# RWKV's three sums over a head (key norm, mean, variance): a pair of rounded products in place of one fp32 product

## The chip, the core and the metric

One core of a Trainium2 chip runs the whole program. The metric is the device time of one execution in microseconds; the kernel before was timed in 3 runs. Every instruction is recorded by the hardware profiler in one further execution.

## The reference, cut to what matters

The program is one inference step of a two-layer streaming encoder for a prompt of 512 tokens and 8 sequences of 16 tokens, 640 tokens in all. Layer 0's mixer runs RWKV-7 time mixing (8 heads of 64) beside forgetting attention (8 heads of 64) on one input projection; an output projection joins them. What the change touches is in RWKV, in three sums over the 64 channels of a head:

```python
    kk = k * k_k.reshape(H_A, HEAD_DIM).astype(jnp.float32)
    kk = kk / jnp.maximum(jnp.sqrt(jnp.sum(kk * kk, axis=-1, keepdims=True)), 1e-12)
...
    y, s_t = wkv7_scan(r, decay, k, v, -kk, kk * a, s0)
    mean = jnp.mean(y, axis=-1, keepdims=True)
    var = jnp.mean(jnp.square(y - mean), axis=-1, keepdims=True)
    y = (y - mean) * lax.rsqrt(var + GN_EPS) * lnx_g.reshape(H_A, HEAD_DIM).astype(jnp.float32) \
        + lnx_b.reshape(H_A, HEAD_DIM).astype(jnp.float32)
```

Everything is fp32. The later layers (a gated convolutional FFN after each mixer, chunk attention beside HGRN2 in layer 1's mixer) are not touched.

## The kernel before, in words

Activations lie with channels on the 128 partitions and tokens along the free axis, in two halves of 320 tokens. A large projection is `linear` (line 362): each weight tile of 128x1024 is loaded, split by ScalarE into a rounded part `whi` (L376) and by VectorE into what remains, `wlo` (L377), and each output tile is the sum of three rounded products per tile of the contraction, (whi, hi), (whi, lo), (wlo, hi), all on line 387 with 320 columns. These L387 products are most of TensorE's work.

Layer 0's mixer is `mixer0` (line 545). Its input projection feeds `evz` (line 893), which collects r, k and v of a pair of heads and then calls `rwkv` (line 617) for that pair and half: 8 items in all, one for each of four pairs `p` and two halves `hf`. An item has three stages. Stage A forms decays, the normed key `kk`, masks and the products `sc`; stage B inverts a triangular system (a part of it on POOL, by way of DRAM); stage C carries the state, makes `y` (tile `Y`, L836), takes its mean and variance, scales it and writes it to DRAM (`ydr`, L888). Each stage has its own ring of buffers of 320 columns, 11 for A, 8 for B and 5 for C (line 624); a buffer is taken when a tile is made and given back after its last reader. The buffer `ABM`, which holds `AR`, `BK` and the masked products of an item, is there twice, so an item uses that of the item two before it.

A sum over a head is a product with a matrix that has ones in two blocks of 64x64 (`blkr`). In `rwkv` it is `m1` (line 634), one fp32 product (L636). Layer 1's HGRN2 takes its one sum by `headsum` (line 224): its caller has ScalarE write the rounded part `sh` (L1383), VectorE subtracts it (`sl`, L226), and two rounded products accumulate (L228).

Attention over the prompt and the samples comes after the input projection in the program, in a lane of its own. Then `out_proj` (line 531) runs twice: first with attention's outputs, then with RWKV's four `ydr` tiles. It reads each tile back (`yb`, L538), rounds it (`yh`, L539) and subtracts (`yl`, L540). The second one does all output tiles for the first half of the tokens, then all for the second half.

No order is written by hand. Code is assigned to lanes with priorities (`k.lane`), and a scheduler lists the instructions of every engine by priority and by when it takes their inputs and buffers to be ready. Each engine then runs its list in that order. A new instruction or a longer lifetime of a buffer can therefore move others.

Of the kernel before, what the change touches and what calls it, by code (L numbers as in the profile page):

```python
# [12 lines left out]
AF = mybir.ActivationFunctionType  # L13
ALU = mybir.AluOpType
# [530 lines left out]
def mixer0(tc, A, k):  # L545
    nc = tc.nc
    V, S, G, T, dma, mm, fm, P, C = k.V, k.S, k.G, k.T, k.dma, k.mm, k.fm, k.P, k.C
    ident, blk1, one = k.ident, k.blk1, k.one
# [8 lines left out]
    with tc.tile_pool(name="mx", bufs=1) as mp:  # L557
# [59 lines left out]
        def rwkv(p, hf, r, kz, v, lrt, grt, item):  # L617
# [5 lines left out]
            def wt(name, w=HF, dt=F32):  # L623
                return mp.tile([128, w], dt, tag="w" + stage[0], name=name, bufs={"A": 11, "B": 8, "C": 5}[stage[0]])

            def hsum(src, t, func, name, **kw):
                hi, lo = wt("hi", dt=F32R), wt("lo", dt=F32R)
                S.activation(hi, src, func, **kw)
                return k.headsum(mm(name, stage[0]), t, hi, lo)
# [4 lines left out]
            def m1(lhsT, rhs, name):  # L634
                ps = mm(name, stage[0])
                T.matmul(ps[:, 0:HF], lhsT, rhs, start=True, stop=True)  # L636
                return ps[:, 0:HF]
# [5 lines left out]
            kk, rn = wt("kk"), wt("rn")  # L643
            V.tensor_scalar(kk, kz, P("k_k", p), None, op0=ALU.mult)
            S.activation(rn, kz, AF.Square, scale=P("k_k", p))
            ps = m1(blk1, rn, "kkn")
            n2, rn = wt("n2"), wt("rn")
            V.tensor_scalar(n2, ps, 1e-24, None, op0=ALU.max)
            S.activation(rn, n2, AF.Ln, scale=float(2 ** 20))
# [32 lines left out]
            for (u0, n, prompt) in (((0, 4, 1), (4, 1, 1)) if hf == 0 else ((0, 3, 1), (3, 2, 0))):  # L682
                for h in range(2):
                    ps = mm("sc", stage[0])
# [59 lines left out]
            ps = mm("trA", stage[0])  # L744
# [4 lines left out]
            ps = mm("trV", stage[0])  # L749
# [7 lines left out]
            for (u0, n) in ((0, 4), (4, 1)):  # L757
                ps = mm("trB", stage[0])
# [18 lines left out]
            ps = mm("U", stage[0])  # L777
# [27 lines left out]
            y = wt("y")  # L805
# [7 lines left out]
            for c in range(npu):  # L813
# [6 lines left out]
                ps = mm("Sn", stage[0])  # L820
# [8 lines left out]
            ps = mm("Y", stage[0])  # L829
# [8 lines left out]
            if hf:  # L838
# [4 lines left out]
                ps = mm("SAs", stage[0])  # L843
# [12 lines left out]
                ps = mm("Ss", stage[0])  # L856
# [9 lines left out]
                ps = mm("Ys", stage[0])  # L866
# [8 lines left out]
                S.copy(y[:, 192:320], ps[:, 0:128])  # L875
                dma(A["o_rw"][:, p], rwo)

            V.scalar_tensor_tensor(y, m1(blk1, y, "mean"), -1.0 / 64, y, op0=ALU.mult, op1=ALU.add)
            sq = wt("sq2")
            S.activation(sq, y, AF.Square)  # L880
            rs = wt("rs")
            S.activation(rs, m1(blk1, sq, "var"), AF.Ln, scale=1.0 / 64, bias=k.gneps)
            S.activation(rs, rs, AF.Exp, scale=-0.5)
            V.tensor_tensor(y, y, rs, op=ALU.mult)
            V.tensor_scalar(y, y, P("lnx_g", p), P("lnx_b", p), op0=ALU.mult, op1=ALU.add)
# [7 lines left out]
        def evz(m, h, ps):  # L893
# [24 lines left out]
            if m == 12:  # L918

                t = o[0:64]  # L920
                V.tensor_scalar(t, t, 2.0, None, op0=ALU.mult)
                sigm(t, t, None)
                V.tensor_scalar(t, t, 2.0, -1.0, op0=ALU.mult, op1=ALU.add)
                cur["lr", h] = o
            elif m == 13:
                sigm(o, o, None)
                cur["g", h] = o
            else:
                cur["rkv"[m // 4], h] = o
                if m >= 8:  # L930
                    with k.lane(0):
                        rwkv(m - 8, h, cur["r", h], cur["k", h], cur["v", h], cur["lr", h], cur["g", h], items[0])
                    items[0] += 1
# [641 lines left out]
```

## Time and profile before

| | us |
|---|---|
| median of 3 runs | 2039.95 |
| lowest, highest run | 2035.65, 2040.83 |
| profiled execution, its own time | 2040.38 |
| its span, first to last instruction | 2038.6 |
| TensorE matmul busy | 1929.7 (95%) |
| VectorE busy | 1215.2 (60%) |
| ScalarE busy | 943.4 (46%) |
| POOL busy | 523.3 (26%) |

In rows, PE is TensorE's matmuls and PEld its weight loads, DVE is VectorE, ACT ScalarE, SP the engine that issues DMAs. L387 is line 387 of the kernel. `mean<-y,blkr` names the tile written and those read. A matmul record lasts longer than its place in the sequence, since matmuls are pipelined; the distance from start to start is what it takes. An fp32 product has two records. PEclk is the granted share of TensorE's full clock of 2.4 GHz; the lower level is 1.2 GHz.

### The profile page before, as it was taken

The page shows a single profiled execution, that of the slowest core. Times are in us where ns is not written, and L with a number is a line of the kernel's source. Part 1 is how long each engine was busy: PE and PEld are TensorE (multiplying, and loading weights), DVE is VectorE, ACT ScalarE, POOL GpSimd, SP SyncE. Part 2 cuts the span into 40 slices and gives each one's busy share as a digit, 9 for nine tenths or more (in the row PEclk, how much of TensorE's full clock was granted, in tenths as well). Part 3 has the DMA queues.
Part 4 walks back from the last instruction along what each step waited for, and adds up shares of the span by engine and source line. Part 5 has one row for each costly group of instructions (what it writes and reads, how often), then busy time and mean ns, then how long its engine had stood idle before and what let it go on. Part 6 is the DMA issues. An engine that isn't in the chain of part 4 may idle for free. (4 is left out here: it accounts for less than half of the span.)

```text
span 2038.6 us, 42518 instructions
## 1 busy us (share of the span) xinstructions
PE 1929.7 (95%) x16860; PEld 1744.6 (86%) x16860; DVE 1215.2 (60%) x2490; ACT 943.4 (46%) x1877; POOL 523.3 (26%) x1090
## 2 busy tenths in 40 slices
PE   6999998989899999999999999998999999999997
PEld 2878777856697899999999888877889999999997
DVE  3755655776676453553558416776668653454456
ACT  4534333544456441441546325655537651452454
POOL 1324354643031120220212202432222321121112
PEclk9999998999999999999999999998999999999998
DMA  9464435466536532222237775455624322222223
GB/s 315 156 215 132 147 116 170 116 160 168 187 119 221 176 100 74 83 65 81 72 120 230 241 227 175 134 148 169 224 87 148 105 81 74 73 68 80 81 81 124
DMA packets 146710, 282.52 MB, mean 139 GB/s; under 512 B 39768, under 2 KB 80064, under 8 KB 146512
## 3 DMA queue, kind: packets, MB, share of 16 engines
q1 hardware_dynamic: 138832, 267.22, 41.2%
q0 software_dynamic: 7680, 12.59, 2.9%
q8 instruction: 133, 2.18, 0.4%
q14 instruction: 65, 0.53, 0.1%
HBM read 247.69 MB, written 32.07 MB: 137 GB/s over the span
## 5 line engine op out<-in xcount | busy, mean ns | idle before, releaser
L387 PE MATMUL lin<-hi,whi 128*128 128x320 f32 x2272 | 717.3, 316 | 12.2 <-ACT whi L376 7.1
L387 PE MATMUL lin<-hi,wlo 128*128 128x320 f32 x2272 | 714.7, 315 | 6.3 <-DVE wlo L377 6.1
L387 PE MATMUL lin<-lo,whi 128*128 128x320 f32 x2272 | 711.8, 313 | 0.0
L377 DVE TENSOR_TENSOR wlo<-wraw,whi 128x1024 fp32r<-128x1024 f32 (+1 forms) x272 | 335.1, 1233 | 352.0 <-ACT whi L376 351.3
L376 ACT CAST whi<-wraw 128x1024 fp32r<-128x1024 f32 (+1 forms) x272 | 279.3, 1027 | 514.9 <-PE lin L387 373.5
L387 PEld LDWEIGHTS lin<-hi,whi 128*128 128x128 f32 x2272 | 431.5, 190 | 37.4 <-ACT whi L376 10.9
L387 PEld LDWEIGHTS lin<-hi,wlo 128*128 128x128 f32 x2272 | 431.7, 190 | 19.4 <-DVE wlo L377 9.6
L387 PEld LDWEIGHTS lin<-lo,whi 128*128 128x128 f32 x2272 | 431.6, 190 | 6.2 <-issue 3.8
L387 PE MATMUL lin<-gh,whi 128*128 128x320 f32 x704 | 218.2, 310 | 2.9 <-ACT whi L376 1.7
L387 PE MATMUL lin<-gl,whi 128*128 128x320 f32 x704 | 217.6, 309 | 0.6 <-DVE gl L479 0.6
L387 PE MATMUL lin<-gh,wlo 128*128 128x320 f32 x704 | 217.5, 310 | 0.6 <-DVE wlo L377 0.5
L461 POOL COPY cvo<-u 128x2 f32<-128x2 f32 x88 | 83.3, 947 | 379.9 <-ACT u L459 379.9
L422 DVE SCALAR_TENSOR_TENSOR x<-lin,ada_cm,x 128x192 f32<-128x192 f32 (+1 forms) x160 | 76.8, 481 | 145.6 <-PE lin L387 145.3
L387 PEld LDWEIGHTS lin<-gh,whi 128*128 128x128 f32 x704 | 132.0, 188 | 4.6 <-ACT whi L376 2.8
L387 PEld LDWEIGHTS lin<-gl,whi 128*128 128x128 f32 x704 | 132.2, 188 | 1.3 <-DVE gl L479 1.1
L387 PEld LDWEIGHTS lin<-gh,wlo 128*128 128x128 f32 x704 | 132.1, 188 | 1.4 <-DVE wlo L377 1.1
L427 POOL TENSOR_TENSOR x<-x,rs 128x128 f32<-128x128 f32 x80 | 49.3, 617 | 310.4 <-DVE rs L425 295.5
L465 DVE SCALAR_TENSOR_TENSOR t<-u,pp,t 128x656 f32<-128x656 f32 x88 | 79.3, 901 | 26.3 <-ACT t L464 25.6
L1324 POOL TENSOR_TENSOR d<-d,q 128x160 f32<-128x160 f32 (+1 forms) x48 | 41.9, 873 | 179.8 <-ACT d L1323 179.8
L387 PE MATMUL lin<-yh,whi 128*128 128x320 f32 x256 | 80.8, 319 | 6.7 <-DVE eL L1288 2.5
L464 ACT ACTIVATE t<-u,pp 128x656 f32<-128x656 f32 x88 | 82.5, 938 | 7.2 <-ACT u L460 0.4
L455 ACT COPY u<-lin 128x320 f32<-128x320 f32 x88 | 37.5, 427 | 96.9 <-PE lin L387 96.9
(396 smaller groups left out, 3114.2 us busy)
## 6 DMA issues: line engine op xcount, KB each, us to landing
wraw<-in_w_up_dram SPq DMA_DIRECT2D x100, 512.0 KB
wada<-in_ada_w_dram SPq DMA_DIRECT2D x96, 512.0 KB
wraw<-in_w_cd_dram SPq DMA_DIRECT2D x44, 512.0 KB
wraw<-in_w_dn_dram SPq DMA_DIRECT2D x48, 448.0 KB
wraw<-in_w_ab_dram SPq DMA_DIRECT2D x40, 512.0 KB
wraw<-in_w_dn_dram SPq DMA_DIRECT2D x16, 512.0 KB
wraw<-in_w_abo_dram SPq DMA_DIRECT2D x12, 512.0 KB
wraw<-in_w_cdo_dram SPq DMA_DIRECT2D x12, 512.0 KB
```

Source lines behind the costliest of these rows:

```text
L376: S.copy(wh[:, :w], r[:, :w])
L377: V.tensor_tensor(wl[:, :w], r[:, :w], wh[:, :w].bitcast(F32), op=ALU.subtract)
L387: T.matmul(ps[:, 0:HF], w[:, (j * nk + kk) * 128:(j * nk + kk + 1) * 128], a(h, kk), start=c == 0, stop=c == 3 * nk - 1)
L422: V.scalar_tensor_tensor(xx[:, :npr], ps[:, :npr], m[:, 16 + o, 0:1], xx[:, :npr], op0=ALU.mult, op1=ALU.add)
L427: G.tensor_tensor(xx[:, npr:], xx[:, npr:], t.rearrange("p b t -> p (b t)"), op=ALU.add)
L455: S.copy(u[:, 2:2 + HF], ps)
L461: G.tensor_copy(cvo[:, o, 0, :], u[:, NP:NP + 2])
L464: S.activation(t, u[:, 2:], AF.Identity, scale=pp[:, ow + 88 + o:ow + 89 + o], bias=pp[:, ob + o:ob + o + 1])
L465: V.scalar_tensor_tensor(t, u[:, 1:UW - 1], pp[:, ow + 44 + o:ow + 45 + o], t, op0=ALU.mult, op1=ALU.add)
L1324: G.tensor_tensor(dv[:, :, h2:], dv[:, :, h2:], xq[:, :, h2:], op=ALU.mult)
```

## The change

The three calls of `m1` with the ones matrix become calls of `hsum` (line 626), a helper that `rwkv` already has: ScalarE writes the rounded part `hi` of the source (for key norm and variance the square, for the mean a copy; L628), VectorE subtracts it from the full value (`lo`, L226), and two products of rounded operands with `blkr` accumulate in the same PSUM tile (L228). `hi` and `lo` are two more tiles of 320 columns from the stage's ring. Key norm is in stage A, mean and variance are in stage C.

```diff
-            ps = m1(blk1, rn, "kkn")
+            ps = hsum(kz, rn, AF.Square, "kkn", scale=P("k_k", p))
...
-            V.scalar_tensor_tensor(y, m1(blk1, y, "mean"), -1.0 / 64, y, op0=ALU.mult, op1=ALU.add)
+            V.scalar_tensor_tensor(y, hsum(y, y, AF.Copy, "mean"), -1.0 / 64, y, op0=ALU.mult, op1=ALU.add)
             sq = wt("sq2")
             S.activation(sq, y, AF.Square)
             rs = wt("rs")
-            S.activation(rs, m1(blk1, sq, "var"), AF.Ln, scale=1.0 / 64, bias=k.gneps)
+            S.activation(rs, hsum(y, sq, AF.Square, "var"), AF.Ln, scale=1.0 / 64, bias=k.gneps)
```

The scheduler's lists differ from the first key norm on. Two places near the end of the mixer follow, and a third behind them.

TensorE around the last item's variance, before. `yh_7010` is the first output projection's rounded input (attention's half); the second one's is `yh_7317`.

```order
L387 MATMUL lin_7078<-yh_7010,wlo_7047 128x320
L387 MATMUL lin_7078<-yh_7010,whi_7046 128x320
L636 MATMUL var_5923<-sq2_5920,blkr_95 128x320
L387 MATMUL lin_7078<-yl_7011,whi_7046 128x320
L387 MATMUL lin_7078<-yh_7010,wlo_7047 128x320
```

TensorE at the same place, of the change. Here the first projection's input is `yh_7130`, the second's `yh_7437`.

```order
L387 MATMUL lin_7525<-yl_7438,whi_7507 128x320
L387 MATMUL lin_7525<-yh_7437,wlo_7508 128x320
L228 MATMUL var_6041<-hi_6038,blkr_95 128x320
L228 MATMUL var_6041<-lo_6039,blkr_95 128x320
L387 MATMUL lin_7545<-yh_7437,whi_7541 128x320
```

The variance has moved from among the first projection's products to among the second's. Before, 267 products of L387 follow it up to the first that reads the last tile of the second half, which this item writes; now it is 67. In the old list 15 of the 24 sums stand ahead of the input projection's last product, in the new one 12 (six key norms, three means, three variances).

ScalarE around the last item's square and logarithm (L880, L882), before: `yh<-yb` are the casts for the output projections, `whi` weight casts, L323 squares of the norm after the mixer.

```order
L875 COPY y<-Ys 128x128
L539 CAST yh<-yb 128x320 x4
L880 ACTIVATE sq_5920<-y 128x320
L539 CAST yh<-yb 128x320 x3
L882 ACTIVATE rs<-var,c_cols 128x320
L539 CAST yh<-yb 128x320
L883 ACTIVATE rs<-rs 128x320
L539 CAST yh<-yb 128x320 x3
L376 CAST whi<-wraw 128x1024 x2
L539 CAST yh<-yb 128x320
```

ScalarE at the same place, of the change:

```order
L875 COPY y<-Ys 128x128
L628 ACTIVATE hi<-y 128x320
L539 CAST yh<-yb 128x320 x2
L376 CAST whi<-wraw 128x1024
L880 ACTIVATE sq_6035<-y 128x320
L628 ACTIVATE hi<-y 128x320
L376 CAST whi<-wraw 128x1024
L882 ACTIVATE rs<-var,c_cols 128x320
L883 ACTIVATE rs<-rs 128x320
L376 CAST whi<-wraw 128x1024 x2
L323 ACTIVATE sq<-x_7124 128x320 x4
L539 CAST yh<-yb 128x320
```

The other yh casts now stand ahead of this item's end, the weight casts of the second projection among its steps, and the last cast behind four squares of the next norm.

SP's queue around the last item's write of y (L888) and its reading back (L538), before:

```order
L538 DMA yb<-ydr_251 128x320
L373 DMA wraw<-in_w_abo_dram 128x1024
L888 DMA ydr_252<-y 128x320
L538 DMA yb<-ydr_252 128x320
L435 DMA cvs<-in_cvs_dram 128x704
L373 DMA wraw<-in_w_abo_dram 128x1024 x5
```

SP at the same place, of the change:

```order
L538 DMA yb<-ydr_251 128x320
L373 DMA wraw<-in_w_abo_dram 128x1024 x2
L373 DMA wraw<-in_w_up_dram 128x1024
L888 DMA ydr_252<-y 128x320
L538 DMA yb<-ydr_252 128x320
L435 DMA cvs<-in_cvs_dram 128x704
```

All of the second projection's weight loads and the first of the FFN now stand ahead of the write; before, five of the projection's stood behind it.

## Rows read from the trace of the kernel before

**Rows 1.** The page, busy us, share of the span and instructions of each engine.

```profile
PE 1929.7 (95%) x16860; PEld 1744.6 (86%) x16860; DVE 1215.2 (60%) x2490; ACT 943.4 (46%) x1877; POOL 523.3 (26%) x1090
```

**Rows 2.** Busy time by stretches of layer 0's mixer: all, then line 387 alone.

```profile
core 0: us, PE busy (x) PEld busy (x) DVE busy (x) ACT busy (x) POOL busy (x), PEclk, DMA share, GB/s
60.00:404.00 344.00, 328.66 (x3458) 269.02 (x3459) 215.33 (x502) 145.35 (x325) 149.93 (x346) 0.98 0.49 151
404.00:572.00 168.00, 149.30 (x1848) 110.54 (x1847) 119.59 (x366) 75.40 (x197) 51.42 (x130) 0.95 0.61 169
...
core 0: us, PE busy (x) PEld busy (x), PEclk, DMA share, GB/s
60.00:404.00 344.00, 205.38 (x1148) 175.26 (x1149) 0.98 0.49 151
404.00:572.00 168.00, 29.96 (x192) 27.95 (x191) 0.95 0.61 169
```

**Rows 3.** Timeline of TensorE, the first mean sum: start us, us, what.

```profile
195.84 0.31 PE L387 MATMUL lin<-lo,whi 128*128 128x320 f32 x1
195.99 0.70 PE L636 MATMUL mean<-y,blkr 128*128 128x320 f32 x2
196.29 0.55 PE L387 MATMUL lin<-hi,wlo 128*128 128x320 f32 x1
196.68 0.31 PE L387 MATMUL lin<-hi,whi 128*128 128x320 f32 x1
```

**Rows 4.** Timeline of TensorE, a rounded sum product in layer 1's mixer.

```profile
1156.50 0.31 PE L387 MATMUL lin<-hi,whi 128*128 128x320 f32 x1
1156.65 0.30 PE L228 MATMUL ms<-sh,blkr 128*128 128x320 f32 x1
1156.79 0.31 PE L387 MATMUL lin<-lo,whi 128*128 128x320 f32 x1
```

**Rows 5.** Groups by line, 1100 to 1600 us: busy us, mean ns | idle before.

```profile
L1383 ACT ACTIVATE sh<-y 128x320 fp32r<-128x320 f32 x8 | 3.6, 456 | 0.0
L226 DVE TENSOR_TENSOR sl<-sq,sh 128x320 fp32r<-128x320 f32 x8 | 3.9, 490 | 2.2 <-ACT sh L1383 2.2
```

**Rows 6.** Waits, 60 to 560 us: us in total, times, longest.

```profile
DVE ABM L672 <- PE Y L836: 8.3, 2, 5.1
```

**Rows 7.** Timeline, from the last item's variance to the second projection's second half.

```profile
545.88 0.70 PE L636 MATMUL var<-sq,blkr 128*128 128x320 f32 x2
546.86 0.52 ACT L882 ACTIVATE rs<-var,c_cols 128x320 f32<-128x320 f32 x1
547.93 0.47 ACT L883 ACTIVATE rs<-rs 128x320 f32<-128x320 f32 x1
548.46 0.49 DVE L884 TENSOR_TENSOR y<-y,rs 128x320 f32<-128x320 f32 x1
550.25 0.44 DVE L885 TENSOR_SCALAR y<-y,pp 128x320 f32<-128x320 f32 x1
552.46 0.48 DVE L886 TENSOR_TENSOR y<-y,bon 128x320 f32<-128x320 f32 x1
554.00 0.48 DVE L887 TENSOR_TENSOR y<-g,y 128x320 f32<-128x320 f32 x1
554.50 0.41 SPq L888 DMA_DIRECT2D ydr<-y  x1
558.22 0.32 SPq L538 DMA_DIRECT2D yb<-ydr  x1
560.45 0.46 ACT L539 CAST yh<-yb 128x320 fp32r<-128x320 f32 x1 [0.74 <-DMA yb<-ydr]
586.77 0.31 PE L387 MATMUL lin<-yh,whi 128*128 128x320 f32 x1
```

**Rows 8.** Busy time by stretches: three spells at a lower granted clock.

```profile
328.10:338.40 10.30, 10.30 (x35) 7.71 (x35) 3.36 (x6) 4.10 (x10) 4.12 (x11) 0.53 0.27 92
451.00:461.20 10.20, 10.20 (x63) 5.31 (x61) 6.46 (x21) 2.19 (x7) 1.76 (x3) 0.53 0.95 240
502.20:509.00 6.80, 6.80 (x95) 4.29 (x92) 5.30 (x15) 3.28 (x8) 0.00 (x0) 0.79 1.23 269
```

## Prediction

> **What bounds the kernel now.** I read the busy shares first, then the stage the change touches, then single instructions, then the way out of that stage. TensorE is the busiest engine by far; VectorE and ScalarE have 40% and more of the span free [rows 1]. The 24 sums all lie in layer 0's mixer, roughly 60 to 602 us, a good quarter of the span. That mixer has two parts. Up to about 404 us the input projection runs: TensorE is busy 329 of 344 us, and the projection's products alone are 205 us of it. From 404 to 572 us attention and the last RWKV items run, with only 192 products of the large projections among them, all of the first output projection; TensorE is busy 149 of 168 us there [rows 2]. That leaves 18.7 us idle, against 15.3 in the twice as long part before. The reader is to see that TensorE is nearly full where projection products fill the gaps, and less so where they run out.
>
> The median of the three runs is 2039.95 us; the profiled execution took 2040.4 (a span of 2038.6 and 1.8 around it), 0.4 above the median. The sum goes against 2040.4. A measurement of this kernel can tell about 0.3% from nothing, 6.1 us.
>
> **TensorE: 24 products out, 48 in.** The first mean sum shows the old price: two projection products and the sum between them take from 195.84 to 196.68, 0.84 us [rows 3]. Products of the same 320 columns in one pass start 0.145 us apart, so the fp32 sum takes 0.84 - 0.29 = 0.55 us. Layer 1 already sums squares in the new way, and there a rounded product takes exactly one such place: the product before starts at 1156.50, the sum at 1156.65, the next at 1156.79 [rows 4]. So a pair costs 0.29 us and each sum saves 0.26. There are 3 sums for each of 8 items (four pairs of heads, two halves): 24 x 0.26 = 6.2 us off TensorE. Bounds: 0 if the stage does not wait for TensorE, 12.4 if all of it ran at half the clock.
>
> Something speaks against the full 6.2. Between 404 and 572 us weight loading is busy 111 of 168 us, two thirds, while matmuls show 149 [rows 2]; so there TensorE may not be the limit. In the PE order of before 15 of the 24 sums stand ahead of the input projection's last product. If only these pay, the term is 15 x 0.26 = 3.9. The Trainium skill (Perfetto Trace Analysis, section Identifying the Most-Contended Engine) says the same as a rule: busy time of matmuls misleads because they are pipelined, and the share of weight loading is to be read. The trace agrees that the two shares differ; whether the tail is free of TensorE, it does not show. I take 6.2, since a pipelined matmul still holds its place and 89% of that part is matmul, and keep 3.9 as a rival.
>
> **ScalarE and VectorE: 24 instructions more on each.** The new roundings cost what layer 1's cost, 0.456 us on ScalarE and 0.490 on VectorE [rows 5]: 24 x 0.456 = 10.9 us and 24 x 0.490 = 11.8 us. As work I cost them at nothing: between 60 and 572 us VectorE is busy 335 of 512 us and ScalarE 221 [rows 2], and meanwhile TensorE has projections or another item. As latency they lengthen each sum by 0.46 + 0.49 - 0.26 = 0.7 us. With that cover gone, and every sum on one chain, it would be 24 x 0.7 = 16.8 us. It is not one chain: an item's AR waits for the Y product of the item two before it, which holds the buffer [rows 6], and Y stands ahead of that item's mean and variance. So these two delay no later item through that buffer. What hi and lo take of the rings of 11 and 5 buffers is no instruction; it shows as order, next. No DMA is added.
>
> **The order moves.** Projections now run ahead of the RWKV items. In the order of before, the last item's variance stands in the first output projection, 267 products ahead of the first one that reads what this item hands on (in the second output projection, second half). In the changed order it stands in the second projection, and 67 products are left. At 0.145 us these are 38.7 and 9.7 us of cover. Under it must fit the way from that sum to the last cast: the sum starts at 545.88, its Ln at 546.86, the last instruction on y at 554.00, its write at 554.50, the read back at 558.22, the cast at 560.45, done at 560.91 [rows 7]: 15.0 us. The pieces alone, without waits between them, are 0.98 + 0.52 + 0.47 + 1.89 (four VectorE steps) + 3.72 + 2.23 + 0.46 = 10.3 us. Before, all of it was hidden: the second half starts only at 586.77 [rows 7]. Now the cover is short by 15.0 - 9.7 = 5.3 us at most and by 0.6 at least. In the old ScalarE order three yh casts stand between the last square and its Ln, now one rounding and one weight cast, so neither end is nearest; I take the middle, 3.0 us. On SP's queue the last write of y stands behind weight loads in both orders, and I put nothing on that; if a load there waits for its buffer, it is part of rival B.
>
> **Sum.** 2040.4 - 6.2 + 3.0 = 2037.2, so **2037 us**, 0.15% less.
>
> **Rivals.** (A) *Faster*: the stage also loses a spell at the slow clock. From 328 and from 451 us the granted clock is 0.53 for 10 us each, about the 1.2 GHz level, and from 502 us 0.79 over 6.8 us [rows 8]. A 10-us spell costs half of itself, 5.1 us. If shorter sums and the new order keep TensorE out of the gap ahead of one, the time is 2037.2 - 5.1 = 2032; with both gone, 2027. For it: both lie in this stage, and each needs one gap. Against: nothing in the change aims at them, and a new gap can bring a new spell.
>
> (B) *Slower*: the last RWKV item ends later than the projections can cover. The cover that shrinks from 267 to 67 products is 200 products, 29 us, that lay beside or behind the last items and now lie ahead of them; by the last product of the input projection RWKV is about one item further behind. After 404 us TensorE already idles 18.7 us [rows 2]. If a third to a half of that filler is not replaced, the stage grows by 9.7 to 14.5 us: 2037.2 + 12 = 2049. From the start of the last instruction on y (554.00) to the cast's end is 6.9 us, and 18 products of the second half can go ahead (2.6 us), so this case decides from the point at which that instruction starts after 586.8 + 2.6 - 6.9 = 582.5 us. The Trainium skill (TensorE: Matmul & The Clock Gate, section HAM oscillation) adds that idle stretches pull TensorE's clock down; the spells of [rows 8] lie in the part with the most idle time, which agrees, and one more of them would be up to 5.1 us. For B: attention starts later against the projection, too. Against: the old chain had 26 us in hand (560.9 to 586.8).
>
> (C) *No gain in the tail*: 2040.4 - 3.9 + 3.0 = 2039.5. That the products do not get cheaper at all is ruled out by [rows 4].
>
> **Chances and range.** The forecast has 0.33 (own range 2034 to 2042), C 0.14; both are within 0.3% of 2039.95 (2033.8 to 2046.1), 0.47 together. A has 0.27, B 0.26. The range goes down to most of two spells lost (2028) and up to B's price with its upper bound (2051).
>
> **What would show it.** Right, step by step: each new product takes 0.145 us between projection products; 24 roundings of 0.46 us on ScalarE and 24 of 0.49 us on VectorE; the input projection's last product 19 to 29 us before 404; the last instruction on y between 565 and 582; in the second half of the second projection a gap of 0.6 to 5.3 us behind its first 18 products; after 602 us the same pattern, shifted. It is wrong if 60 to 602 us changes by more than 6 us either way: then the granted clock (A) or the start of the last instruction on y (B) tells which.

## The result, and the profile after

| | before | changed |
|---|---|---|
| median of 5 runs each, us | 2039.95 | 2053.03 |
| lowest, highest run | 2032.11, 2041.17 | 2046.33, 2061.61 |
| ratio, 95% interval | | 1.0077 [1.0050, 1.0104] |
| profiled execution, its span | 2040.38, 2038.6 | 2061.61, 2059.8 |

The changed kernel is slower by 13 us; forecast were 3 us less, and the range ended at 2051. The profiled execution is the longest of the five, 8.6 us above their median, so stretches of its trace show some us more than the median lost.

The page's busy times against [rows 1]:

```profile
PE 1940.3 (94%) x16860; PEld 1751.3 (85%) x16860; DVE 1225.2 (59%) x2514; ACT 953.7 (46%) x1901; POOL 519.2 (25%) x1090
```

The added work is there (24 instructions more on VectorE and on ScalarE, 10 us each), and no engine comes near TensorE. Windows of the changed kernel, against [rows 2]:

```profile
core 0: us, PE busy (x) PEld busy (x) DVE busy (x) ACT busy (x) POOL busy (x), PEclk, DMA share, GB/s
60.00:404.00 344.00, 324.23 (x3346) 264.31 (x3345) 213.67 (x495) 146.04 (x325) 139.63 (x321) 0.98 0.49 151
404.00:572.00 168.00, 152.02 (x1859) 111.72 (x1859) 121.76 (x373) 82.54 (x216) 60.60 (x139) 0.96 0.56 160
572.00:619.00 47.00, 40.11 (x311) 36.79 (x311) 33.01 (x68) 19.61 (x36) 10.18 (x27) 0.93 0.33 108
```

The same view of the kernel before, the end of its mixer:

```profile
572.00:602.00 30.00, 29.64 (x200) 29.12 (x199) 23.73 (x47) 18.29 (x31) 9.24 (x11) 1.00 0.38 123
```

Up to 572 us both kernels fill TensorE alike. What follows, the second output projection, fills it for 29.6 of 30 us before, and for 40 of 47 us in the changed kernel. To place this I counted L387 products by their start; the input projection has the first 1248, attention's output projection the next 192, RWKV's the last 192 of the mixer:

```
start of L387 product, us     1248th  1440th  1537th  1554th  1555th  1632nd   L887, last item
before                         404.2   572.5   586.8   589.3   589.4   601.8   554.0
changed                        377.1   571.7   598.4   600.9   603.7   618.5   596.6
```

The input projection ends 27 us earlier, attention's output projection 0.8 earlier, and then 17.5 us are lost (12.5 between the 1440th and the 1537th product and 5.0 after the 1554th), so that the mixer ends 16.7 us later. Another 4.5 of the spans' 21.2 us come behind it, most of them by 677 us, in layers that are the same in both. The two places, in the timeline of the changed kernel (start us, us, engine, what, idle time and releaser):

```profile
573.62 0.56 PE L836 MATMUL Y<-ABM,St 64*64 64x64 f32 x12
574.71 1.15 PE L851 MATMUL SAs<-S,W1m 64*64 64x64 f32 x32 [0.53 <-ACT y L837]
577.11 1.56 PE L862 MATMUL Ss<-Sm,ABM 128*64 128x256 f32 x8 [1.25 <-DVE Sm L860]
579.45 0.45 PE L869 MATMUL Ys<-ABM,SAV 128*64 128x64 f32 x8 [0.78 <-DVE rwo L865]
579.83 1.11 PE L873 MATMUL Ys<-ABM,S 64*64 64x16 f32 x32
581.53 0.64 PE L387 MATMUL lin<-yl,whi 128*128 128x320 f32 x1 [0.59 <-DVE yl L540]
...
591.54 0.52 ACT L882 ACTIVATE rs<-var,c_cols 128x320 f32<-128x320 f32 x1
593.27 0.48 DVE L884 TENSOR_TENSOR y<-y,rs 128x320 f32<-128x320 f32 x1
596.62 0.48 DVE L887 TENSOR_TENSOR y<-g,y 128x320 f32<-128x320 f32 x1
597.13 0.41 SPq L888 DMA_DIRECT2D ydr<-y  x1
600.89 0.31 PE L387 MATMUL lin<-yh,wlo 128*128 128x320 f32 x1
600.91 0.33 SPq L538 DMA_DIRECT2D yb<-ydr  x1
603.15 0.46 ACT L539 CAST yh<-yb 128x320 fp32r<-128x320 f32 x1 [2.20 <-DMA yb<-ydr]
603.66 0.56 PE L387 MATMUL lin<-yh,whi 128*128 128x320 f32 x2 [2.46 <-ACT yh L539]
```

First, the last item's state steps (L836 to L873) stand in TensorE's queue at the start of the second projection's products: 8 us with hardly a product, 3 of them idle until a step on another engine is done. Second, the 1555th product waits for the last item's cast. Behind both waits the granted clock is down for a while, at the 1.2 GHz level from 581.5 us and at 0.88 on average behind the second; before, it is 1.00 there:

```profile
581.50:584.60 3.10, 3.07 (x11) 3.07 (x12) 2.38 (x6) 1.04 (x3) 0.00 (x0) 0.50 0.36 106
603.70:618.50 14.80, 13.92 (x79) 13.07 (x80) 11.93 (x27) 8.28 (x15) 8.04 (x17) 0.88 0.32 110
```

```profile
589.40:601.80 12.40, 12.04 (x81) 11.64 (x80) 11.17 (x27) 9.46 (x18) 4.46 (x7) 1.00 0.38 127
```

So of the 5.0 us, 2.6 are the wait, and 2.4 come behind it, where the products run slower. Both places are one thing, the last RWKV item being late: L887 starts at 596.62, where [rows 7] have 554.00. The way from there to the cast is as before, 6.5 us; the rounded products cost what [rows 4] promised (the key norm's first one in the changed kernel):

```profile
87.05 0.31 PE L387 MATMUL lin<-hi,wlo 128*128 128x320 f32 x1
87.20 0.31 PE L228 MATMUL kkn<-hi,blkr 128*128 128x320 f32 x1
87.34 0.31 PE L387 MATMUL lin<-hi,whi 128*128 128x320 f32 x1
```

The items' ends (start of L887 for the eight items) show that every item is late, by 19 us at the first, 31 at the second, 20 to 31 at the next five, and 43 at the last:

```
before    206.7  254.8  312.8  370.6  423.4  475.2  519.2  554.0
changed   226.0  286.0  343.5  396.7  448.5  506.1  539.0  596.6
```

### The profile page after: what moved, and what is told of

Read it like the earlier page. It is cut to its first block, busy times and chain, and to the rows that moved or that the text cites. A ratio compares the mean times of both kernels' runs of the same rounds, so it can differ in the third digit from the quotient of the medians.

```text
span 2059.8 us, 42570 instructions
## 1 busy us (share of the span) xinstructions
PE 1940.3 (94%) x16860; PEld 1751.3 (85%) x16860; DVE 1225.2 (59%) x2514; ACT 953.7 (46%) x1901; POOL 519.2 (25%) x1090
## 5 line engine op out<-in xcount | busy, mean ns | idle before, releaser
L387 PE MATMUL lin<-hi,whi 128*128 128x320 f32 x2272 | 715.6, 315 | 16.5 <-DVE f L1053 8.6
L387 PE MATMUL lin<-hi,wlo 128*128 128x320 f32 x2272 | 712.9, 314 | 10.4 <-DVE wlo L377 10.2
L387 PE MATMUL lin<-lo,whi 128*128 128x320 f32 x2272 | 710.1, 313 | 1.0 <-DVE lo L352 1.0
L387 PEld LDWEIGHTS lin<-hi,whi 128*128 128x128 f32 x2272 | 430.7, 190 | 40.0 <-DVE f L1053 12.9
L387 PEld LDWEIGHTS lin<-hi,wlo 128*128 128x128 f32 x2272 | 430.6, 190 | 24.5 <-DVE wlo L377 14.4
L387 PEld LDWEIGHTS lin<-lo,whi 128*128 128x128 f32 x2272 | 430.7, 190 | 6.3 <-issue 2.9
L387 PE MATMUL lin<-gh,whi 128*128 128x320 f32 x704 | 219.7, 313 | 2.7 <-ACT whi L376 1.5
L387 PE MATMUL lin<-gl,whi 128*128 128x320 f32 x704 | 218.9, 311 | 0.6 <-DVE gl L479 0.6
L387 PE MATMUL lin<-gh,wlo 128*128 128x320 f32 x704 | 218.4, 311 | 0.6 <-DVE wlo L377 0.5
L387 PEld LDWEIGHTS lin<-gh,whi 128*128 128x128 f32 x704 | 133.2, 189 | 4.5 <-ACT whi L376 2.7
L387 PEld LDWEIGHTS lin<-gl,whi 128*128 128x128 f32 x704 | 133.4, 189 | 1.3 <-DVE gl L479 1.1
L387 PEld LDWEIGHTS lin<-gh,wlo 128*128 128x128 f32 x704 | 133.1, 189 | 1.2 <-DVE wlo L377 1.1
L387 PE MATMUL lin<-yh,whi 128*128 128x320 f32 x256 | 83.4, 328 | 5.5 <-ACT yh L539 2.5
```

The source lines that it names most:

```text
L387: T.matmul(ps[:, 0:HF], w[:, (j * nk + kk) * 128:(j * nk + kk + 1) * 128], a(h, kk), start=c == 0, stop=c == 3 * nk - 1)
```

## The experiments

Theories. **B**: the mixer ends at the later of two ends, TensorE's (attention's output projection) and the last item's; as a rule, the 1632nd product starts at the later of the 1440th + 29.3 us and the last L887 + 22 us, two distances taken from the first runs and then used on the others. Against it **W**, the added work costs time wherever it stands, and **C**, every delay of RWKV's chain costs. For why the last item is late: **L**, the latency of the added steps; **R**, the buffers that `hi` and `lo` hold; **O**, the written order, which any edit moves; later **Q**, **S** and **V**, queueing behind projections on VectorE, SP, or for the buffers of tag f. Every kernel was timed in 5 rounds against the kernel before; ratios are to that. The kernel before then had medians of 2034.84 to 2038.19, while the forecasts count from 2039.95, so a time is held against a forecast by what it adds to its own before. A ratio is estimated from all runs of both and is not quite that of the two medians.

### Parts of the change alone

kkn_only keeps the new sum in the key norm, meanvar_only in mean and variance. The two cuts are against the changed kernel, first a line of kkn_only (the variance's is turned back likewise), then that of meanvar_only:

```diff
-            V.scalar_tensor_tensor(y, hsum(y, y, AF.Copy, "mean"), -1.0 / 64, y, ...)
+            V.scalar_tensor_tensor(y, m1(blk1, y, "mean"), -1.0 / 64, y, ...)
...
-            ps = hsum(kz, rn, AF.Square, "kkn", scale=P("k_k", p))
+            ps = m1(blk1, rn, "kkn")
```

> Only the key norm's 8 sums are made the new way; mean and variance keep the fp32 product. Theory L (latency: rounding and subtraction lengthen the chain of every item, 0.7 us a sum and what queues behind them): the key norm stands at the head of each item, so about half of the 13 us or more: 2045 to 2050 us, and the last instruction on y (L887) of the last item starts 15 to 30 us later than before's 554.0. Theory R (buffers: the two tiles are held in the ring of 11 in which the key norm's stage lies): nearly all of the loss comes from here, 2050 to 2056, L887 at 585 to 600. Theory O (order: the written order lets projection products run ahead of RWKV's, whatever the cause): its order has the last variance 1464 projection products in (before 1279, changed kernel 1488), so L887 at 585 to 597 and 2046 to 2054.

> Only mean and variance (16 sums) are made the new way; the key norm keeps the fp32 product. Theory L: two sums one behind the other at an item's end, which only the last item pays: 2 x 0.7 = 1.4 us later, less 4.2 us of products: 2036 to 2041. Theory R: the two tiles lie in the ring of 5 of the last stage; little loss, 2036 to 2043. Theory O: the last variance stands 1392 projection products in, 113 later than before's 1279 and 96 earlier than the changed kernel's 1488: L887 of the last item at 565 to 580 us, still covered (the limit worked out from before's trace is 582.5), so 2036 to 2042. If it is as slow as the changed kernel (2050 or more), the loss is not the key norm's.

Measured: kkn_only 2040.47, ratio 1.0015 [0.9996, 1.0033], L887 of the last item at 583.0; meanvar_only 2039.59, 1.0013 [0.9990, 1.0037], L887 at 574.7. Neither part costs what the whole does. The lateness of the parts is as large as that of the whole (29 and 21 us; the whole 43), their time is not: that is B, with 26 us in hand before anything is lost. All three of L, R and O priced the key norm too high; for mean and variance they agreed on the time, and O alone had L887 (565 to 580), where L had 1.4 us.

### The steps without the cheaper product, and the cheaper product without the steps

steps_fp32 makes rounding and a VectorE step, then the fp32 product of the second tile; hi_only has the Square write its result rounded and sums that, and leaves the remaining part out (shown for the variance; the key norm likewise):

```diff
-                return k.headsum(mm(name, stage[0]), t, hi, lo)
+                V.scalar_tensor_tensor(lo, hi.bitcast(F32), 0.0, t, op0=ALU.mult, op1=ALU.add)
+                return m1(blk1, lo, name)
...
-            sq = wt("sq2")
+            sq = wt("sq2", dt=F32R)
...
-            S.activation(rs, m1(blk1, sq, "var"), AF.Ln, scale=1.0 / 64, bias=k.gneps)
+            S.activation(rs, m1(blk1.bitcast(F32R), sq, "var"), AF.Ln, scale=1.0 / 64, bias=k.gneps)
```

> All 24 sums keep the fp32 product of before, but the rounding on ScalarE and an instruction on VectorE that reads it and t are made ahead of each, with the same two tiles; the product reads the second tile, so the latency is that of the changed kernel without the cheaper product. Theories L and R: as slow as the changed kernel or 6 us slower, 2052 to 2060, L887 of the last item at 590 us or later. Theory O: set by its own order, in which the last variance stands 1392 products in, 96 earlier than in the changed kernel: L887 at 570 to 585 and 2040 to 2047.

> Key norm and variance are summed in one rounded product written by the Square that is there anyway, so no instruction and no tile is added; the remaining part of these two is left out of the sum. The mean keeps the fp32 product. TensorE has 16 x (0.55 - 0.145) = 6.5 us less to do. Theories L and R: nothing is added, so no loss: 2033 to 2040, L887 of the last item at or before 554. Theory O: its order has the last variance 1464 products in, nearly as late as the changed kernel (1488; before 1279), although no step was added: L887 at 580 to 597 and 2042 to 2053.

Measured: steps_fp32 2049.45, 1.0053 [1.0030, 1.0076], L887 at 579.4; hi_only 2039.21, 1.0004 [0.9984, 1.0024], L887 at 585.4. By the prices of [rows 3] and [rows 4] hi_only has 6.5 us less of TensorE's work, with nothing added; no gain can be seen, and the last item came 31 us late although no item had a step more. L and R had it at or before 554; O had the place, and the time lies between the forecasts. steps_fp32, 11.7 us above its own before, lies between them too, with L887 where O had it, and is slow on the other end: its 1440th product starts at 582.6, 10 us later than before.

### Buffers, and neutral changes of the order

changed_rings: rings 11 and 5 become 9 and 7. changed_swap and early6_swap exchange the two lines that begin an item, before_swap two of the key norm's; early6_swap also returns to the fp32 sum for items 6 and 7:

```diff
-            sigm(s, m1(w2a2[0:64, cs_], lrt[0:64], "w2"), P("w0", p))
             sigm(a, m1(w2a2[64:128, cs_], lrt[64:128], "a2"), P("a0", p))
+            sigm(s, m1(w2a2[0:64, cs_], lrt[0:64], "w2"), P("w0", p))
...
+                if item >= 6:
+                    return m1(blk1, t, name)
```

> The changed kernel with two buffers fewer in the ring of the key norm's stage (11 to 9) and two more in that of mean and variance (5 to 7). The written order comes out the same on all five engines. Theory R (the two tiles of each sum take buffers that later work waits for): either end of it moves: the smaller ring costs 3 us or more on the key norm's side, the larger one gives back part of the 13 us on the other: outside 2049 to 2057. Theories L (latency of the two added steps) and O (order): nothing changes, the time of the changed kernel, 2053 within 4.

> The changed kernel with the two lines that begin an item (decay and a, independent of each other) in the other order; all sums as in the changed kernel, the same instructions, the same steps in each sum. Theory L: the latency of each sum is the same, so 2050 to 2056. Theory O: the written order decides; in this one the third to sixth key norm stand 22, 40, 19 and 35 projection products earlier than in the changed kernel, the last variance at the same place (1488): L887 of the last item 5 to 15 us earlier than 596.6, so 2040 to 2049.

> The kernel before (fp32 sums) with two independent lines of the key norm (the scaled key on VectorE, its square on ScalarE) in the other order; the work is the same to the instruction. Theory L: the same time as before, 2036 to 2041, and the last item's L887 at 554 within 5. Theory O: the order moves all the same: the last variance stands 1416 projection products in (before 1279), so L887 of the last item 10 to 25 us later, at 564 to 580; below the limit of 582.5, so that the time may stay within 6 us of before, on either side.

> The new sums in the first six items only, while projections still keep TensorE busy, the fp32 sums in the last two, whose chain is not covered; the item's first two lines swapped as in changed_swap. Theory L: the last two items are as fast as before, the first six are hidden behind projections, and 18 x 0.26 = 4.7 us of products are saved: 2033 to 2038. Theory O: the last variance stands 1464 products in; L887 of the last item at 570 to 585, near the limit: 2036 to 2043.

Measured: changed_rings 2054.31, 1.0086 [1.0061, 1.0111], no different from the changed kernel; a loss in one ring and a gain in the other that cancel are not excluded. More against R are kkn_only, far below its price, and hi_only, whose items come late with no tile added. changed_swap 2052.29, 1.0073 [1.0049, 1.0098], as L had it and not O: this shift of the order changed nothing. But before_swap, the same work to the instruction, took 2043.68, 1.0036 [1.0016, 1.0055], with the last L887 at 571.4, where O had it: an order can by itself cost 0.2 to 0.5%. B does not explain that cost: in before_swap's trace the 1632nd product comes 1.4 us earlier than before, and the profiled execution is 5.8 us below the kernel's median, so where its 7 us lie is not shown. early6_swap, 2048.15, 1.0048 [1.0028, 1.0068], missed both forecasts: its last L887 is at 591.0 though the last two items are those of before.

### The end of the last item alone

before_delay28 and before_delay56 lengthen the last item of the kernel before, by 28 and 56 multiplications with 1.0; changed_lastcut leaves out mean, variance and normalisation of the last item of the changed one. The cut is before_delay56's:

```diff
-            V.tensor_tensor(y, y, bon, op=ALU.add)
+            [G.tensor_scalar(y, y, 1.0, None, op0=ALU.mult) for _ in range(56 if item == 7 else 0)]; V.tensor_tensor(y, y, bon, op=ALU.add)
```

> The kernel before (fp32 sums) with 28 multiplications of y by 1.0 on GpSimd, one behind the other, in the last item alone, ahead of its last instructions (the GpSimd steps of this shape take 0.5 to 1 us, so 14 to 28 us); TensorE's order is that of before up to the second output projection. Theory B (the stage ends at the later of two ends: TensorE's 1440th projection product + 29.3 us, or the last item's L887 + 22 us, as all runs so far have it): before has 26 us in hand, so with L887 at 568 to 582 the time is that of before within 4 us. Theory W (the added work on ScalarE and VectorE costs time wherever it stands): no work is added there, the same time. Theory C (every delay of RWKV's chain costs): 14 to 28 us more, 2051 to 2066.

> As before_delay28 with 56 multiplications in the last item: 28 to 56 us. Theory B: the time rises by L887 + 22 - 601.8, no more: with L887 at 597, where the changed kernel has it, by 17 us (2055); with L887 at 610 by 30. Theory W: no work is added on ScalarE or VectorE, so the time of before within 4 us. Theory C: 28 to 56 us more than before.

> The changed kernel without mean, variance and normalisation in the last of the eight items (this part of the computation is left out), all else with its new sums. Theory B: L887 of the last item 10 to 16 us earlier than 596.6, and the stage ends as much earlier, until TensorE's own end binds: 2039 to 2045. Theory W: 2 of 24 sums less, 2 us less: 2050 to 2053. Theory C as B.

A multiplication took 1.01 us, the upper end of what I allowed, but one starts 1.09 to 2.2 us after the other, with other GpSimd work between the first 28. Those took 40 us, and so before_delay28 came to the changed kernel's place, past the 568 to 582 for which B had no loss; B's rule is applied to the place that was met. Its timeline:

```profile
595.57 0.49 DVE L887 TENSOR_TENSOR y<-g,y 128x320 f32<-128x320 f32 x1
600.62 0.90 PE L387 MATMUL lin<-yh,whi 128*128 128x320 f32 x2 [7.12 <-ACT yh L539]
```

That of before_delay56:

```profile
620.69 0.49 DVE L887 TENSOR_TENSOR y<-g,y 128x320 f32<-128x320 f32 x1
621.21 0.33 SPq L888 DMA_DIRECT2D ydr<-y  x1
623.00 0.33 SPq L538 DMA_DIRECT2D yb<-ydr  x1
625.19 0.46 ACT L539 CAST yh<-yb 128x320 fp32r<-128x320 f32 x1 [37.34 <-DMA yb<-ydr]
625.70 0.90 PE L387 MATMUL lin<-yh,whi 128*128 128x320 f32 x2 [37.60 <-ACT yh L539]
```

The 1632nd product follows L887 by 20.4 us in both (616.0 and 641.1), so by B the mixer ends 14 and 39 us after before's 601.8; the medians rose by 12.0 (2046.79, 1.0072 [1.0047, 1.0096]) and 39.0 (2073.84, 1.0191 [1.0161, 1.0221]). L887 was 42 and 67 us late: by C the time would have risen as much, by W not at all. With L887 where the changed kernel has it, and all fp32 sums, before_delay28 loses what the change loses. It loses it in one place, though: its state steps are early, and the 1555th product waits 7.1 us. So the changed kernel's two losses do not simply add: without the first, TensorE would have stood longer at the second.

changed_lastcut (L887 at 581.4) took 2045.87, 1.0063 [1.0041, 1.0086]. That is 11.0 us above its own before, where B had 5 at most; by the time alone it can't be told from the changed kernel, and W's 10 to 13 would fit. Its 1555th product waits no more, but the first place stays: 26 us from the 1440th to the 1537th product, since the last item's state steps are as late as in the changed kernel. Late state steps thus cost time by themselves, which B's rule leaves out, and that the loss goes when the changed kernel's last item alone is made early is not shown.

### Where the items queue

lo_pool has the subtraction on GpSimd, changed_actq issues the projection's writes from ScalarE's queue, changed_f4 gives tag f, the tiles in which the projection's q, k and v and their parts leave, four buffers for two and takes two from the ring of 11 (not in the cut); before_actq and before_f4 are the last two edits without the change, lo_pool_actq and lo_pool_f4 join them:

```diff
-        def headsum(ps, t, hi, lo):
+        def headsum(ps, t, hi, lo, E=None):
...
-            V.tensor_tensor(lo, t, hi.bitcast(F32), op=ALU.subtract)
+            (E or V).tensor_tensor(lo, t, hi.bitcast(F32), op=ALU.subtract)
...
-                return k.headsum(mm(name, stage[0]), t, hi, lo)
+                return k.headsum(mm(name, stage[0]), t, hi, lo, G)
...
-                dma(A["o_fk" if i == 1 else "o_fv"][p][:, hs], o)
+                S.dma_start(A["o_fk" if i == 1 else "o_fv"][p][:, hs], o)
...
-            o = mp.tile([128, HF], F32, tag="f", name="f", bufs=2)
+            o = mp.tile([128, HF], F32, tag="f", name="f", bufs=4)
```

What led there is the first item. Of its 19.3 us, about 1.2 lie ahead of its start, 1.5 at the key norm, 0.8 at the mean and 3.0 at the variance; 12.8 lie between AR (92.1 and 95.2 us) and the copy of Y (192.8 and 208.7), where it has no new instruction. VectorE in the changed kernel there, and then SP:

```profile
108.25 0.29 DVE L691 TENSOR_TENSOR ABM<-sc,c_mp 128x128 f32<-128x128 f32 x1
111.90 0.49 DVE L1053 SCALAR_TENSOR_TENSOR f<-lin,f 128x320 fp32r<-128x320 f32 x1 [3.36 <-DMA fks<-f]
112.31 0.24 DVE L693 TENSOR_REDUCE Cc<-ABM 64x16 f32<-64x64 f32 x1
```

```profile
113.54 0.38 SPq L703 DMA_DIRECT2D d<-Cc  x1
...
118.81 0.34 SPq L946 DMA_DIRECT2D out_dram<-f  x1
119.20 0.42 SPq L948 DMA_DIRECT2D fv<-f  x1
119.72 0.34 SPq L705 DMA_DIRECT2D At<-d  x1
```

SP in the kernel before:

```profile
105.94 0.37 SPq L703 DMA_DIRECT2D d<-Cc  x1
...
109.36 0.32 SPq L705 DMA_DIRECT2D At<-d  x1
...
119.14 0.34 SPq L946 DMA_DIRECT2D out_dram<-f  x1
```

The item's reduction L693 stands behind a projection's split that waits 3.36 us for a buffer, and its read back L705 behind the writes of k and v. Before, both stood ahead of them. Queued in this order, an item that is 3 us late at AR is 7.6 late at its first DMA (L703) and 12.7 at the read of TB (L721).

> The changed kernel with the 24 subtractions on GpSimd instead of VectorE (a longer instruction, about 0.8 us for 0.49, on an engine that has little to do in this stage). Theory Q (an item is late because its added steps queue behind projections' instructions on VectorE): the first item's end comes 5 to 10 us earlier than 226.0, L887 of the last at 575 to 587: 2040 to 2046. Theory L (the latency of the added steps itself): 24 x 0.3 us longer, so as late or later: 2052 to 2058.

> The changed kernel with the writes of q, k and v of the projection (L943, 946, 948, 950) issued from ScalarE's queue, behind the copy that makes them, instead of SP's. Theory S (items queue in SP behind these writes, which wait for ScalarE): the first item's TB read (L721) starts at 127 to 133 instead of 137.8, its end is at 212 to 219 instead of 226; L887 of the last item at 570 to 588; 2038 to 2047. Theory V (they queue on VectorE behind splits that wait for the buffers of f): unchanged, TB at 137 or later, 2050 to 2056. Theory L (the latency of the sums alone): unchanged.

> The changed kernel with four buffers instead of two for the parts of q, k, v (tag f), at the price of two buffers of the ring of 11, which changed_rings showed to be free. Theory V: the waits of L1053 for a DMA on f go, the first item's first DMA (L703) starts at 107 to 110 instead of 113.5, its end at 212 to 220; L887 of the last item at 570 to 590; 2038 to 2048. Theory S: the DMA starts earlier, but TB not before 134; 2048 to 2056. Theory L: 2050 to 2056.

> The kernel before with the same writes on ScalarE's queue. By theory B the stage of before ends on TensorE's side (26 us in hand on RWKV's), so an earlier item is worth nothing: 2032 to 2040, L887 of the last item at or before 554. If the attention's inputs come earlier too, the 1440th product comes earlier and the time falls below 2032.

> The kernel before with four buffers for the tag f. Theory B: the stage ends at the later of the 1440th product + 29.3 and L887 + 22 (20.4 in the two delay runs). Its order has the last variance 1464 products in (before 1279), so L887 at 565 to 585 and the projection ends earlier (381 or so for 404): 2030 to 2040. Theory V without B: items shorter, so earlier than before: 2025 to 2032.

> All 24 sums the new way, subtractions on GpSimd, writes of q, k and v from ScalarE's queue. Theory A (the causes add): 2041.8 - 4 = 2036 to 2039, the first item's end at 213 to 219, L887 of the last at 565 to 580 and the 1440th product at 563 to 570. Theory T (the last item is late because projections that end early bring attention forward against it, however early the first items are): L887 of the last item still at 580 to 590, 2040 to 2046.

> All 24 sums the new way, subtractions on GpSimd, four buffers for tag f and nine in the ring of 11. Theory A: 2041.8 - 4 = 2035 to 2039, the first item's end at 208 to 215, L887 of the last item at 565 to 580. Theory T: the first item is early, the last one still at 580 to 590, 2040 to 2048.

All runs with their medians, that of their own before, the first item's end, and the ends that B compares (profiled execution of each):

```
                 median   before   ratio [95%]               L887 of item   product start    L387 product
                                                             first   last   1248th  1440th   1632nd
before           2039.95                                     206.7   554.0   404.2   572.5   601.8
before_swap      2043.68  2036.30  1.0036 [1.0016, 1.0055]   212     571.4   401.2   570.6   600.4
before_actq      2037.35  2038.19  1.0005 [0.9988, 1.0021]   211     540.3   394.4   572.5   601.8
before_f4        2042.81  2038.19  1.0031 [1.0015, 1.0046]   209     583.9   372.8   563.3   605.9
before_delay28   2046.79  2034.84  1.0072 [1.0047, 1.0096]   206     595.6   406.0   576.5   616.0
before_delay56   2073.84  2034.84  1.0191 [1.0161, 1.0221]   210     620.7   403.8   571.1   641.1
hi_only          2039.21  2037.76  1.0004 [0.9984, 1.0024]   215     585.4   377.9   568.5   608.2
kkn_only         2040.47  2037.76  1.0015 [0.9996, 1.0033]   219     583.0   371.9   564.4   605.7
meanvar_only     2039.59  2037.76  1.0013 [0.9990, 1.0037]   208     574.7   388.1   577.4   606.6
steps_fp32       2049.45  2037.76  1.0053 [1.0030, 1.0076]   223     579.4   378.8   582.6   611.9
early6_swap      2048.15  2036.30  1.0048 [1.0028, 1.0068]   225     591.0   374.2   574.1   613.4
changed          2053.03  2039.95  1.0077 [1.0050, 1.0104]   226.0   596.6   377.1   571.7   618.5
changed_swap     2052.29  2036.30  1.0073 [1.0049, 1.0098]   225     598.0   378.0   572.9   620.1
changed_rings    2054.31  2036.30  1.0086 [1.0061, 1.0111]   225     589.4   372.8   565.7   611.0
changed_lastcut  2045.87  2034.84  1.0063 [1.0041, 1.0086]   226     581.4   375.5   568.5   609.7
changed_actq     2049.59  2038.19  1.0054 [1.0032, 1.0076]   220     584.9   368.4   564.4   606.5
changed_f4       2048.74  2038.19  1.0053 [1.0034, 1.0071]   213     587.5   372.9   562.4   609.6
lo_pool          2041.75  2034.84  1.0027 [1.0007, 1.0047]   223     583.5   370.4   568.9   605.9
lo_pool_actq     2050.38  2038.08  1.0055 [1.0032, 1.0077]   218     585.3   364.7   579.1   610.4
lo_pool_f4       2038.77  2038.08  1.0011 [0.9993, 1.0029]   209     579.7   361.9   576.6   606.4
```

A profile is one execution and can lie 11 to 13 us off its kernel's median (changed_actq: 2038.63 against 2049.59; before_delay28: 2059.41 against 2046.79); the trace columns show places, the medians times. The medians rose above their own before by what the 1632nd product came later, within 5 us, but for changed_rings, before_swap and changed_actq (7 to 9 us more), whose profiles are 6 to 11 us below their medians. Three readings. The 1632nd product lies within 1 us of the later of (1440th + 29.3) and (last L887 + 22) in all rows but four: before_delay28 and before_delay56 follow L887 by 20.4, and lo_pool_actq and changed_lastcut exceed the bound by 2 and 6 us, the latter for the reason told above. V held for the early items: in changed_f4 the first DMA starts at 108.2 as forecast and the first item ends 13 us earlier, at 213; by S (changed_actq) it ends 6 us earlier, with the TB read at 135.4, between the two forecasts. Yet the last item gained only 9 to 12 us by either, and both kernels came out beyond the slow end (2048.74 for 2038 to 2048, 2049.59 for 2038 to 2047); their intervals overlap the changed kernel's, so that a gain in time is not shown. before_f4 took 3 us more than forecast, 5 against its own before. lo_pool is clearly faster than the changed kernel (1.0027 against 1.0077), but its first item came only 3 us earlier, so that Q's account of it is not shown. The two joins went apart: lo_pool_f4 is even with before, A's time in us and T's lower end against its own before; lo_pool_actq missed both forecasts, late on TensorE's side.

So the early lateness explains part of the last item's: 21 of its 43 us are there at its start (L645, 435.1 and 456.4 us), 33 at the first of its three state steps (L822). Another 11 come between the first step and the third. Changed kernel, then before:

```profile
556.01 0.34 PE L822 MATMUL Sn<-SAV,ABM 128*64 128x64 f32 x4
563.97 0.34 PE L822 MATMUL Sn<-SAV,ABM 128*64 128x64 f32 x4
571.93 0.34 PE L822 MATMUL Sn<-SAV,ABM 128*64 128x64 f32 x4
```

```profile
523.29 0.34 PE L822 MATMUL Sn<-SAV,ABM 128*64 128x64 f32 x4 [0.19 <-DVE SAV L811]
525.61 0.34 PE L822 MATMUL Sn<-SAV,ABM 128*64 128x64 f32 x4
528.45 0.34 PE L822 MATMUL Sn<-SAV,ABM 128*64 128x64 f32 x4
```

In the changed kernel 96 products of the first output projection stand between the first and the third in TensorE's list, before none. This part is the order's: hi_only, with no step added, has 84 there and takes 14.4 us, meanvar_only 16 and 6.1.

The lateness goes with the input projection's end: wherever it came before 380 us, the last L887 stands at 579 or later, in before_f4 too, where no sum is changed; where it came at 388 or later, with no delay put in, at 575 or earlier. That fits the order, in which projections go ahead, attention starts earlier, and the last items share the engines with it. No run held the projection back with all else equal, so it stays open whether this is the cause of what is left.

## Why the prediction was wrong

**What came as forecast.** The pair costs 2 x 0.145 us. VectorE's subtraction takes 0.484 to 0.49; ScalarE's rounding 0.457 for mean and variance, 0.547 for the key norm, which has a scale. The input projection's last product came 27 us earlier (19 to 29 forecast). 18 products of the second half went ahead of the last item's cast, and the 1555th waited 2.6 us, within the 0.6 to 5.3 forecast.

**The step that failed** is "the order moves", 3.0 us between 0.6 and 5.3. It took the last item's place in TensorE's order and put its 15 us behind the variance, as if the item itself kept its time and only its cover shrank. The item came 42.6 us later, L887 at 596.6, past the 582.5 from which rival B decides, and B is what happened. The wait the term described is there, 2.6 us at the 1555th product; the larger loss, 12.5 us, lies ahead of it, where I had nothing: the last item's state steps in TensorE's queue at the head of the second projection. In place of 3.0 us the two places lose 17.5 in the trace. Had the state steps been early, the wait would have been the longer, as in before_delay28: the end follows L887. B's 2049 was under-priced, since it counted idle filler and not where the late item's steps stand; the range ended 2 us below the result.

**What stood behind it:** "as work I cost them at nothing", and as latency no chain through the items. Whether the chain through ABM was rightly excluded did not come to matter: the first item lost 5.3 us at its sums (three times 0.7 forecast) and 12.8 where nothing was added. Queues hold part of that, SP's, put at nothing, among them: changed_f4 and changed_actq end the first item 13 and 6 us earlier. Why the last item loses more than the others is shown for 11 us (its state steps among products) and open for the rest.

**-6.2 on TensorE.** True as work, but no gain in time came of it: attention's output projection ends 0.8 us earlier in the changed kernel, and hi_only, with 6.5 us less, ends it 4.0 us earlier and the mixer 6.4 us later, on the last item's side. Rival C, no gain in the tail, was too kind by this. The rule of the Trainium skill (Perfetto Trace Analysis, section Identifying the Most-Contended Engine), that matmul busy time misleads and the share of weight loading is to be read, points the same way here: in the changed kernel weight loading is busy 112 of the 168 us up to 572, matmuls 152, so TensorE has more room there than its matmul share tells. That a chain through other engines sets the end it does not say; the delays show it.

**Rival A.** The spells from 328 and 451 us are gone, as A wanted, but others came; the mean granted clock is 0.97 from 60 to 602 us before and from 60 to 619 us in the changed kernel. (The spell from 328 us lay in the part up to 404 us, which is the fuller one: only two of the three in [rows 8] lie in the part with more idle time, as rival B has it of all.) In the changed kernel:

```profile
500.00:527.70 27.70, 24.61 (x343) 17.90 (x344) 21.00 (x74) 16.52 (x46) 8.99 (x31) 0.98 0.41 133
527.70:537.90 10.20, 5.02 (x42) 4.11 (x40) 4.67 (x11) 1.31 (x3) 1.62 (x2) 0.55 0.27 69
```

Ten us at about the 1.2 GHz level follow a stretch in which matmuls were busy 24.6 of 27.7 us, and in them matmuls are busy 5 of 10.2; a spell lost in one place was found in another.

## What to carry to other kernels

Where two chains end in one stage, look for both ends and for the time in hand on each: an item that ends 14 us earlier on the side that does not end last brought nothing (before_actq), and two edits that can't be told from free alone (1.0013 and 1.0015 here) can together cost 0.8%, when they use up the same reserve. In queues that run in a written order, a few us of latency can grow where instructions of other work now stand ahead; read the items' steps one by one, the first's and the last's, those without a new instruction too. And an order moved by two exchanged lines cost 0.2 to 0.5% in one case and nothing in the other, so a small edit is not to be judged without such a control.

## What the runs showed that I had not expected

The changed sums can be had at a cost that can't be told from nothing: with subtractions on GpSimd (0.88 to 0.98 us each for VectorE's 0.49), four buffers for tag f and two fewer in the first ring, lo_pool_f4 takes 2038.77 us, 1.0011 [0.9993, 1.0029], and its first item ends at 209 us. No version beat the kernel before; before_actq, whose last item ends 14 us earlier, is even with it (1.0005 [0.9988, 1.0021]), since its end is TensorE's. And a rounding with a scale from a column takes ScalarE 0.547 us where one without takes 0.457, for the same 320 columns:

```profile
L628 ACT ACTIVATE hi<-y x16: 452/457/487, 209.2 to 588.1; 128x320 fp32r<-128x320 f32 x16
L628 ACT ACTIVATE hi<-zs,pp x8: 546/547/551, 83.7 to 457.8; 128x320 fp32r<-128x320 f32 x8
```
